# Two edits to a 256-frame hybrid encoder trunk: five weight low parts a layer on GpSimd, and one slice of projections between the sparse branch's output and its split

## The chip, the core and the metric

The kernel runs on one core of one Trainium2 chip. The metric is the device time of one execution in microseconds. The core has five engines with a queue each, served in order: TensorE (PE; PEld is its weight load), VectorE (DVE), ScalarE (ACT), GpSimd (POOL) and SyncE (SP), which issues most DMAs. An instruction waits on semaphores for what it needs; whatever stands behind it in its queue waits too.

## The reference

Two layers over x of 256 x 1024 in float32. A layer normalises x, projects it with one matrix `w_in`, feeds three token mixers (A: gated linear attention, GLA; B: sparse attention over 64 keys chosen by an indexer, DSA; C: differential attention), multiplies each by a SiLU gate, projects each to 1024, merges them by sigmoid gates and adds an output projection to x.

```python
proj = h @ w_in[l]
(gq, gk, gv, ga, gz, bq, bk, bv, iq, ik, iw, bz,
 cq, ck, cv, cz, gate) = jnp.split(proj, SPLIT_AT, axis=-1)
y_a = _gla(...) * jax.nn.silu(gz)
y_b = _dsa(...) * jax.nn.silu(bz)
y_c = _diff(...) * jax.nn.silu(cz)
g = jax.nn.sigmoid(gate.reshape(B, T, N_BRANCH, D_MODEL))
merged = sum(g[:, :, i] * (y @ w_br[l, i]) for i, y in enumerate((y_a, y_b, y_c)))
x = x + merged @ w_out[l]
```

## The kernel before, in words

Every product is made to float32 precision from three matmuls (`mm3`, line 279): each operand is split into a high part that TensorE reads exactly and a low part, the rest; high by high, high by low and low by high are summed in PSUM. A matmul is recorded under lines 124 (products) and 127 (transposes).

Weights come in units of 128 x 1024 (two row blocks of 512 columns). `Stream` (line 184) keeps their order, one list `PLAN` per layer, made from `ORDER` (line 35): bq, cq, ck, gate2, cz, bk, cv, gq, iq, bv, gv, gz, bz, gate0, gate3, gate4, then `br0`, the pair gate5 and gate1 (seven products `q1` to `q7`, by a scheme that saves one of eight), `br1` and the output. Each of the plain projections has four units. `load` (line 199) has SP fetch a unit into one of four `raw` buffers; `split` (line 227) makes the unit's high part `whi` on ScalarE and its low part `wlo` on VectorE, each in one of six buffers. So a raw buffer is loaded again when both parts are made, and a `whi` buffer is written again when TensorE has done the unit six before. Some units of the pair are sums of two, made by DMAs that GpSimd issues (line 211).

`project` (line 344) runs a projection unit by unit: for each half unit it issues the matmuls for both blocks of 128 frames (six, or a slice), and then `flow.pump()` (line 259). `Flow` holds the mixers' work as generators; each `yield n` in one says that its next piece is issued n slices later. So a generator's work is spread between the projections' matmuls. What comes of this is only the order in which the program is written: a scheduler then sets each engine's queue, by that order and by its own estimate of what is ready when.

A projection's accumulators, one for each block of frames, stand in four PSUM buffers called `pj`; what the mixers make in PSUM stands in four others, `at`. The gates' accumulators come free by a tanh on ScalarE (line 1102).

The parts that the argument touches, in the order of a layer's stage from gz to br0:

- `dsa_attend` (line 699): logits `blog`, on VectorE masked by `ns` (line 709) and reduced to the negative row maximum `negm` (711), exponentials `bp` with row sums on ScalarE (678), then a reciprocal `rs` and four scalings on VectorE (717, 720), transposes `pT` on TensorE and their split `bpT` (730, 731).
- `gla_task` (line 875): its output `go` is squared on ScalarE (905), normalised by GpSimd's `v` and `r` (286, 287), scaled by VectorE to `ya` (912), and transposed and split (`yT`, `yTh`, `yTl`).
- `dsa_out` (line 735): two products `av`, each scaled by `bz` to `yb` on VectorE (747) and split to `ybh` (ScalarE) and `ybl` (VectorE).
- `branches` (line 951): `br0` projects the three mixers' outputs in the order A, C, B.

Of the kernel before, what the change touches and what calls it, by code (L numbers as in the profile page):

```python
# [8 lines left out]
F32 = mybir.dt.float32  # L9
F32R = mybir.dt.float32r  # L10
BF16 = mybir.dt.bfloat16
AF = mybir.ActivationFunctionType
# [38 lines left out]
PLAN, USE = [], {}  # L51
# [28 lines left out]
plan()  # L80
NPLAN = len(PLAN)
SUMS_AHEAD = 10


def columns(*widths):
# [21 lines left out]
def trunk(ctx: ExitStack, tc: tile.TileContext, x0, x1, units, wsmall, pack, ptmp, wa2b, out):  # L107
    nc = tc.nc
    V, A, G = nc.vector, nc.scalar, nc.gpsimd
# [32 lines left out]
    def w2(shape, dt=F32, n="w2"):  # L142
        return sp.tile(shape, dt, tag="w2", bufs=BUFS["w2"], name=nm(n))
# [16 lines left out]
    def at(shape, n="at"):  # L160
        return pp.tile(shape, F32, tag="at", bufs=4, name=nm(n))
# [8 lines left out]
    HV = [slice(h * 512, h * 512 + 512) for h in range(2)]  # L170
# [13 lines left out]
    class Stream:  # L184
# [42 lines left out]
        def split(self):  # L227
            j = len(self.made)
            self.begin_sum(j + SUMS_AHEAD)
            raw, (hi, lo) = self.raws[j], self.tiles()  # L230
            self.splits[j] = (A.activation(hi, raw, AF.Copy), V.tensor_sub(lo, raw, hi.bitcast(F32)))  # L231
            what, *arg = PLAN[j % NPLAN]
            if what in ("t1", "t2"):
                self.add(j // NPLAN, "t2" if what == "t1" else "t4", *arg)
            if j in self.after:
                self.hold(j, self.after[j])
# [42 lines left out]
    def mm3(ps, lh, ll, rh, rl, first, last):  # L279
        TE.matmul(ps, lh, rh, start=first, stop=False)  # L280
        TE.matmul(ps, lh, rl, start=False, stop=False)
        TE.matmul(ps, ll, rh, start=False, stop=last)
# [132 lines left out]
    def yT(y):  # L415
        ps = at([P, 4, P], "yT")
        for b in range(4):
            TE.transpose(ps[:, b], y[:, b * P:(b + 1) * P], ident)
        return [[a[:, k] for k in range(4)] for a in split(ps, [P, 4, P], "yT", kp)]
# [117 lines left out]
    for l in range(L):  # L537
# [151 lines left out]
        def transposed_probs(pt, h0, per, t, pT):  # L689

            ps = at([P, per, t + 1, P], "pT")
            for j in range(per):
                for s in range(t + 1):
                    TE.transpose(ps[:, j, s], pt[:, j, s * P:(s + 1) * P], ident)
            hi, lo = split(ps, [P, per, t + 1, P], "pT")
            for j in range(per):
                pT[h0 + j] = [(hi[:, j, s], lo[:, j, s]) for s in range(t + 1)]
# [37 lines left out]
        def dsa_out():  # L735

            his, los = [], []
            for hp in range(2):
                o = at([P, 2, T], "av")
                for j in range(2):  # L740
                    h = 2 * hp + j
                    hs = slice(h * P, h * P + P)
                    v = [(a[:, hs] for a in val["bv"][s]) for s in range(2)]
                    mm3(o[:, j], *v[0], *(a[:, h] for a in bpT[0]), True, False)
                    mm3(o[:, j, P:], *v[1], *(a[:, h] for a in bpT[1]), False, True)
                y = w2([P, CH], F32, "yb")
                V.scalar_tensor_tensor(y, o.rearrange("p j t -> p (j t)"), 0.5, val["bz"][hp], op0=OP.mult, op1=OP.mult)
                hi, lo = split(y, [P, CH], "yb", kp)
                his.append(hi.rearrange("p (j t) -> p j t", j=2))
                los.append(lo.rearrange("p (j t) -> p j t", j=2))  # L750
                yield 1
            for t in range(2):
                yTs[1, t] = [[a[h // 2][:, h % 2, tts[t]] for h in range(4)] for a in (his, los)]
                flow.done.add(f"y1{t}")

        def dsa_task():
            flow.start(dsa_out(), Y["by"], {"bp0", "bp1", "bv", "bz"})
            yield from dsa_index(0)
            flow.start(dsa_attend(0), Y["att0"], {"bq0", "bk0"})
            yield from dsa_index(1)  # L760
            flow.start(dsa_attend(1), Y["att0"], {"bq1", "bk0", "bk1"})
# [355 lines left out]
        for h, n, t in ((0, 0, 0), (0, 0, 1), (0, 1, 0), (0, 1, 1), (1, 0, 0), (1, 1, 0), (1, 0, 1), (1, 1, 1)):  # L1117
# [3 lines left out]
            for ps, c in cols:  # L1121
                for k in range(4):
                    wh, wl = ws.need(use(l, f"out{n}{h}")[k // 2])
                    hi, lo = mT[h, t]
# [90 lines left out]
```

## Time and profile before

| | before |
|---|---|
| median of 3 runs | 601.38 us (601.23 to 602.41) |
| the profiled execution | 602.52 us |
| its span, first to last instruction | 600.8 us |
| mean granted TensorE clock in it | 0.996 |
| TensorE busy with matmuls | 590.5 us (98%) |
| VectorE, ScalarE, GpSimd busy | 476.5, 366.9, 78.6 us |

Times in the rows below are microseconds from the span's start. The busy time of TensorE is a union of intervals that overlap, since a matmul's shown duration (0.39 us for 512 columns) is longer than the distance to the next. So a stop of TensorE is best read from the distance of two starts. A wait is put down to what ended last before it.

### The profile page before, as it was taken

To read this page: it belongs to the slowest core of one execution; us is meant where nothing else is said; L and a number is where in the kernel's file an instruction comes from. 1 tells how busy PE (TensorE), PEld (TensorE's weight loads), DVE (VectorE), ACT (ScalarE), POOL (GpSimd) and SP (SyncE) were. 2 spreads that over 40 slices of the span, in tenths; PEclk is the share of its full clock that TensorE was granted. 3 is DMA by queue.
4 is the path that set the end of the run, shared out by engine and by line. 5 is a ranking of instruction groups with operands and counts; after the bars stand their busy time and mean duration, and the time that the engine had idled before them with its cause. 6 is when DMAs were issued, how large, how long until landed. Compare 5 with 4: busy or idle time off the path is not lost. (4 is left out here: it accounts for less than half of the span.)

```text
span 600.8 us, 8806 instructions
## 1 busy us (share of the span) xinstructions
PE 590.5 (98%) x3142; PEld 500.8 (83%) x3142; DVE 476.5 (79%) x785; ACT 366.9 (61%) x633; POOL 78.6 (13%) x111
## 2 busy tenths in 40 slices
PE   8999999999999998999999999999999999899997
PEld 4888888998899887888878888889888988788886
DVE  6878997766999865899586799676879987679971
ACT  5759875765736555764566788576674545558630
POOL 6034101000011112100010240201000021101000
PEclk9999999999999999999999999999999999999999
DMA  8664566434535997877546455632636198869621
GB/s 343 212 230 141 153 218 190 142 107 173 175 107 195 281 269 161 203 252 239 179 129 208 156 168 166 221 128 90 212 107 207 59 310 303 181 194 238 208 85 71
DMA packets 31148, 111.35 MB, mean 185 GB/s; under 512 B 3456, under 2 KB 3840, under 8 KB 31104
## 3 DMA queue, kind: packets, MB, share of 16 engines
q1 hardware_dynamic: 28800, 102.39, 51.1%
q0 software_dynamic: 2304, 8.39, 8.1%
q8 instruction: 25, 0.41, 0.3%
q14 instruction: 19, 0.16, 0.1%
HBM read 109.72 MB, written 1.05 MB: 184 GB/s over the span
## 5 line engine op out<-in xcount | busy, mean ns | idle before, releaser
L231 ACT ACTIVATE whi<-raw 128x1024 fp32r<-128x1024 f32 x176 | 185.1, 1063 | 110.1 <-issue 25.4
L231 DVE TENSOR_TENSOR wlo<-raw,whi 128x1024 fp32r<-128x1024 f32 x176 | 213.6, 1226 | 41.9 <-ACT whi L231 40.7
L124 PE MATMUL gate<-whi,hTh 128*128 128x512 f32 x128 | 50.7, 396 | 0.7 <-ACT gate L1102 0.7
L124 PE MATMUL gate<-wlo,hTh 128*128 128x512 f32 x128 | 50.7, 396 | 0.0
L124 PE MATMUL gate<-whi,hTl 128*128 128x512 f32 x128 | 49.5, 390 | 0.0
L287 POOL TENSOR_TENSOR r<-v,half 128x4 f32<-128x4 f32 (+1 forms) x24 | 33.7, 1406 | 2.0
L286 POOL TENSOR_SCALAR v<-ss 128x4 f32<-128x4 f32 (+1 forms) x24 | 8.0, 335 | 174.0 <-DVE ss L389 99.5
L211 POOL DMA_DIRECT2D sum<-in_units x16 | 14.2, 888 | 120.7 <-DMA sum<-in_units 55.9
L124 PEld LDWEIGHTS gate<-whi,hTh 128*128 128x128 f32 x128 | 24.1, 188 | 6.2 <-ACT gate L1102 1.6
L124 PE MATMUL br<-whi,yTh 128*128 128x512 f32 x64 | 25.1, 393 | 3.4 <-ACT gate L1102 3.4
L124 PEld LDWEIGHTS gate<-whi,hTl 128*128 128x128 f32 x128 | 24.1, 188 | 4.8
L124 PEld LDWEIGHTS gate<-wlo,hTh 128*128 128x128 f32 x128 | 24.1, 188 | 4.4
L124 PE MATMUL out<-whi,mTh 128*128 128x512 f32 (+1 forms) x72 | 26.7, 371 | 0.0
L124 PE MATMUL out<-wlo,mTh 128*128 128x512 f32 (+1 forms) x72 | 26.3, 366 | 0.0
L124 PE MATMUL out<-whi,mTl 128*128 128x512 f32 (+1 forms) x72 | 26.2, 366 | 0.0
L124 PE MATMUL br<-wlo,yTh 128*128 128x512 f32 x64 | 24.9, 390 | 0.0
L124 PE MATMUL br<-whi,yTl 128*128 128x512 f32 x64 | 24.9, 389 | 0.0
L231 DVE TENSOR_TENSOR wlo<-sum,whi 128x1024 fp32r<-128x1024 f32 x16 | 19.2, 1219 | 5.0 <-ACT whi L231 5.0
L231 ACT ACTIVATE whi<-sum 128x1024 fp32r<-128x1024 f32 x16 | 17.0, 1061 | 9.1 <-PE br L124 5.7
L124 PE MATMUL iq<-hTh,whi 128*128 128x256 f32 x64 | 18.7, 292 | 0.0
L124 PE MATMUL iq<-hTl,whi 128*128 128x256 f32 x64 | 18.4, 288 | 0.0
L124 PE MATMUL bz<-hTh,whi 128*128 128x256 f32 x64 | 18.4, 287 | 0.0
(351 smaller groups left out, 1682.8 us busy)
## 6 DMA issues: line engine op xcount, KB each, us to landing
raw<-in_units SPq DMA_DIRECT2D x180, 512.0 KB, 4.2
sum<-in_units POOLq DMA_DIRECT2D x16, 512.0 KB, 7.2
sum<-in_units SPq DMA_DIRECT2D x8, 512.0 KB, 5.7
wsr<-in_wsmall SPq DMA_DIRECT2D x2, 416.0 KB, 7.7
xe<-in_x SPq DMA_DIRECT2D x1, 584.0 KB, 3.4
x<-in_x SPq DMA_DIRECT2D x1, 512.0 KB, 7.7
out<-xe SPq DMA_DIRECT2D x2, 256.0 KB, 2.2
pt<-in_ptmp SPq DMA_DIRECT2D x1, 384.0 KB, 9.2
```

The lines of the kernel that those rows point to most:

```text
L124: return self.put(nc.tensor.matmul(*a, **k))
L211: G.dma_start(self.sums[l, "t3" if what == "t3" else "t1", pair, i], units[u + i], accum_op=OP.add)
L231: self.splits[j] = (A.activation(hi, raw, AF.Copy), V.tensor_sub(lo, raw, hi.bitcast(F32)))
L286: G.tensor_scalar(v, ss, 1.0 / dim, EPS, op0=OP.mult, op1=OP.add)
L287: G.tensor_tensor(r, v, half[:, :n], op=OP.pow)
```

## The change

There are two edits. In `split`, for five units of each layer (the second of gz, bz, gate0 and gate3, the first of gate4) the low part is made by GpSimd in two halves of 512 columns, instead of by VectorE in one. In `dsa_out` a `yield 1` stands between the scaling `yb` and its split, so that the split is written a slice of projections later. The second edit also puts the whole second product of `dsa_out` a slice later.

```diff
+POOL_LO = [USE[c][i] for c, i in (("gz", 1), ("bz", 1), ("gate0", 1), ("gate3", 1), ("gate4", 0))]
...
-            self.splits[j] = (A.activation(hi, raw, AF.Copy), V.tensor_sub(lo, raw, hi.bitcast(F32)))
             what, *arg = PLAN[j % NPLAN]
+            a = A.activation(hi, raw, AF.Copy)
+            if j % NPLAN in POOL_LO:
+                self.splits[j] = (a,)
+                for h in HV:
+                    G.tensor_sub(lo[:, h], raw[:, h], hi[:, h].bitcast(F32))
+            else:
+                self.splits[j] = (a, V.tensor_sub(lo, raw, hi.bitcast(F32)))
...
                 V.scalar_tensor_tensor(y, o.rearrange("p j t -> p (j t)"), 0.5, val["bz"][hp], op0=OP.mult, op1=OP.mult)
+                yield 1
                 hi, lo = split(y, [P, CH], "yb", kp)
```

The lines behind the edits move down by 5 to 12 in the changed kernel (1102 becomes 1114). The scheduler's order changes in three places of each layer. The number behind a name tells one buffer from the next; it is a few higher in the changed kernel for the same thing.

The first place is ScalarE's queue while TensorE ends gate3. `gate_2425<-gate_546` is the tanh of gate0's first block, `gate_2427` of its second. Before:

```order
L231 ACTIVATE whi_1829<-raw_1827 128x1024
L231 ACTIVATE whi_1853<-raw_1851 128x1024
L730 ACTIVATE bpT_228<-pT_2211 128x4x128
L678 ACTIVATE bp_2354,sums_2325<-blog_2345,negm_2326 128x256 x2
L293 ACTIVATE yTh_2404<-yT_2399 128x512
L1102 ACTIVATE gate_2425<-gate_546_2311 128x512
L231 ACTIVATE whi_1887<-raw_1885 128x1024
L1102 ACTIVATE gate_2427<-gate_547_2312 128x512
L730 ACTIVATE bpT_228<-pT_2442 128x2x128
```

With the change:

```order
L237 ACTIVATE whi_1834<-raw_1832 128x1024
L689 ACTIVATE bp_2359,sums_2330<-blog_2350,negm_2331 128x256 x2
L304 ACTIVATE yTh_2409<-yT_2404 128x512
L237 ACTIVATE whi_1858<-raw_1856 128x1024
L741 ACTIVATE bpT_228<-pT_2216 128x4x128
L1114 ACTIVATE gate_2430<-gate_546_2316 128x512
L1114 ACTIVATE gate_2432<-gate_547_2317 128x512
L237 ACTIVATE whi_1892<-raw_1890 128x1024
L741 ACTIVATE bpT_228<-pT_2447 128x2x128
```

The exponentials and `yTh` moved ahead of one split and of `bpT`, and the second tanh ahead of another. On TensorE, at the same place, the transposes of the probabilities and of `ya` stood twenty matmuls into gate4 (before):

```order
L124 MATMUL gate_597_2567<-whi_1829,hTh 128x512
L124 MATMUL gate_597_2567<-wlo_1830,hTh 128x512
L127 MATMUL pT_2442<-xe,bp_2336 128x128 x4
L127 MATMUL pT_2457<-xe,bp_2354 128x128 x4
L127 MATMUL yT_2510<-xe,ya_2266 128x128 x4
L124 MATMUL gate_598_2568<-whi_1720,hTh 128x512
```

and stand now between gate3 and gate4 (`gate_593` is gate4's first accumulator here):

```order
L129 MATMUL gate_572_2435<-wlo_1707,hTh 128x512
L129 MATMUL gate_572_2435<-whi_1706,hTl 128x512
L132 MATMUL pT_2447<-xe,bp_2341 128x128 x4
L132 MATMUL pT_2462<-xe,bp_2359 128x128 x4
L132 MATMUL yT_2515<-xe,ya_2271 128x128 x4
L129 MATMUL gate_593_2553<-whi_1724,hTh 128x512
```

They moved ahead by twenty matmuls; the number of instructions up to the end of br0 is the same.

The second place is ScalarE's queue at the end of gate4. `gate_571` and `gate_572` are gate3's accumulators, `gate_597` and `gate_598` (now `gate_593` and `gate_594`) gate4's. Before:

```order
L231 ACTIVATE whi_2021<-sum_1678 128x1024
L293 ACTIVATE ybh_2534<-yb_2532 128x512
L293 ACTIVATE ybh_2559<-yb_2557 128x512
L231 ACTIVATE whi_2058<-sum_1699 128x1024
L1102 ACTIVATE gate_2563<-gate_571_2429 128x512
L1102 ACTIVATE gate_2565<-gate_572_2430 128x512
L1102 ACTIVATE gate_2639<-gate_597_2567 128x512
L1102 ACTIVATE gate_2641<-gate_598_2568 128x512
```

With the change:

```order
L304 ACTIVATE ybh_2545<-yb_2537 128x512
L1114 ACTIVATE gate_2549<-gate_571_2434 128x512
L1114 ACTIVATE gate_2551<-gate_572_2435 128x512
L304 ACTIVATE ybh_2588<-yb_2580 128x512
L237 ACTIVATE whi_2026<-sum_1682 128x1024
L1114 ACTIVATE gate_2644<-gate_593_2553 128x512
L237 ACTIVATE whi_2063<-sum_1703 128x1024
L1114 ACTIVATE gate_2646<-gate_594_2554 128x512
```

Gate3's two tanhs moved between the two splits of `yb`, and the splits of the summed units behind them.

The third place is GpSimd's queue during gate0 and gate3. `wlo_1664` and `wlo_1725` are the low parts of gate3's and gate4's unit, `v` and `r` the two GLA normalisers. Before:

```order
L674 MEMSET ns_1897 64x64
L211 DMA sum_1678<-in_units 128x1024
L211 DMA sum_1699<-in_units 128x1024
L286 TENSOR_SCALAR v_2200<-ss_2194 128x4
L287 TENSOR_TENSOR r_2201<-v_2200,half 128x4
L674 MEMSET ns_2235 64x64
L286 TENSOR_SCALAR v_2260<-ss_2254 128x4
L287 TENSOR_TENSOR r_2261<-v_2260,half 128x4
```

With the change:

```order
L685 MEMSET ns_1902 64x64
L241 TENSOR_TENSOR wlo_1664<-raw_1661,whi_1663 128x512 x2
L216 DMA sum_1682<-in_units 128x1024
L216 DMA sum_1703<-in_units 128x1024
L297 TENSOR_SCALAR v_2205<-ss_2199 128x4
L298 TENSOR_TENSOR r_2206<-v_2205,half 128x4
L685 MEMSET ns_2240 64x64
L241 TENSOR_TENSOR wlo_1725<-raw_1722,whi_1724 128x512 x2
L297 TENSOR_SCALAR v_2265<-ss_2259 128x4
L298 TENSOR_TENSOR r_2266<-v_2265,half 128x4
```

Two pairs of halves were put in, one ahead of the DMAs of the sums, one ahead of the second normaliser. SP's order is the same in both kernels.

## Rows read from the trace of the kernel before

**Rows 1.** The page, busy time by engine, share of the span, count of instructions.

```profile
PE 590.5 (98%) x3142; PEld 500.8 (83%) x3142; DVE 476.5 (79%) x785; ACT 366.9 (61%) x633; POOL 78.6 (13%) x111
```

**Rows 2.** Waits of TensorE: total us, times, longest us.

```profile
PE br L124 <- ACT gate L1102: 3.4, 2, 1.7
PE gate L124 <- ACT gate L1102: 0.7, 2, 0.4
```

**Rows 3.** Timeline, TensorE, layer 0: start, duration, instruction [idle before, releaser].

```profile
210.81 0.39 PE L124 MATMUL gate<-whi,hTl 128*128 128x512 f32 x1
211.56 0.50 PE L124 MATMUL gate<-whi,hTh 128*128 128x512 f32 x1 [0.36 <-ACT gate L1102]
211.90 0.40 PE L124 MATMUL gate<-wlo,hTh 128*128 128x512 f32 x1
...
226.53 0.39 PE L124 MATMUL gate<-whi,hTl 128*128 128x512 f32 x1
228.60 0.50 PE L124 MATMUL br<-whi,yTh 128*128 128x512 f32 x1 [1.68 <-ACT gate L1102]
```

**Rows 4.** Timeline, ScalarE, ahead of the first stop.

```profile
208.08 1.06 ACT L231 ACTIVATE whi<-raw 128x1024 fp32r<-128x1024 f32 x1 [1.67 <-PE gate L124]
209.04 0.58 ACT L730 ACTIVATE bpT<-pT 128x512 fp32r<-128x512 f32 x1
209.52 0.47 ACT L678 ACTIVATE bp<-blog,negm 128x256 f32<-128x256 f32 x1
...
210.42 0.60 ACT L293 ACTIVATE yTh<-yT 128x512 fp32r<-128x512 f32 x1
210.90 0.61 ACT L1102 ACTIVATE gate<-gate 128x512 f32<-128x512 f32 x1
```

**Rows 5.** Timeline, ScalarE, ahead of the second stop.

```profile
225.02 0.63 ACT L293 ACTIVATE ybh<-yb 128x512 fp32r<-128x512 f32 x1 [1.89 <-DVE yb L747]
...
227.97 2.04 ACT L1102 ACTIVATE gate<-gate 128x512 f32<-128x512 f32 x4
```

**Rows 6.** Groups by shape: count, busy us, mean ns of one, idle before.

```profile
L231 DVE TENSOR_TENSOR wlo<-raw,whi 128x1024 fp32r<-128x1024 f32 x176 | 213.6, 1226 | 41.9 <-ACT whi L231 40.7
...
L483 POOL TENSOR_TENSOR wlo<-raw,whi 128x512 fp32r<-128x512 f32 x2 | 2.8, 1420 | 1.7 <-ACT whi L479 1.7
...
L287 POOL TENSOR_TENSOR r<-v,half 128x4 f32<-128x4 f32 x16 | 18.2, 1135 | 1.3
```

**Rows 7.** Timeline, SP's load behind gate4's low part; ScalarE's split after it.

```profile
198.75 0.33 SPq L206 DMA_DIRECT2D raw<-in_units  x1
...
199.85 1.06 ACT L231 ACTIVATE whi<-raw 128x1024 fp32r<-128x1024 f32 x1 [2.38 <-DMA raw<-in_units]
```

**Rows 8.** Timeline, TensorE's transposes in gate3 and gate4.

```profile
208.06 0.60 PE L127 MATMUL yT<-xe,ya 128*128 128x128 f32 x4
...
216.27 1.03 PE L127 MATMUL pT<-xe,bp 128*128 128x128 f32 x8
...
217.50 0.48 PE L124 MATMUL gate<-whi,hTh 128*128 128x512 f32 x1
```

**Rows 9.** Timeline, VectorE from a low part to the scaled probabilities.

```profile
204.81 1.22 DVE L231 TENSOR_TENSOR wlo<-raw,whi 128x1024 fp32r<-128x1024 f32 x1
...
208.31 0.69 DVE L711 TENSOR_REDUCE negm<-blog 128x2 f32<-128x512 f32 x1
...
211.66 1.13 DVE L720 TENSOR_SCALAR bp<-bp,rs 128x256 f32<-128x256 f32 x4
```

**Rows 10.** Timeline, GpSimd and VectorE side by side.

```profile
170.88 1.09 POOL L1111 TENSOR_TENSOR gz<-gz,pk 128x512 f32<-128x512 f32 x1 [3.21 <-DVE gz L412]
...
171.31 1.74 DVE L231 TENSOR_TENSOR wlo<-raw,whi 128x1024 fp32r<-128x1024 f32 x1
```

**Rows 11.** Timeline, VectorE and TensorE: a later unit, made and first used.

```profile
249.96 1.22 DVE L231 TENSOR_TENSOR wlo<-sum,whi 128x1024 fp32r<-128x1024 f32 x1
...
255.25 0.39 PE L124 MATMUL q<-wlo,sh 128*128 128x512 f32 x1
```

## The prediction

> **What bounds the kernel now.** I read the page first: TensorE is busy 590.5 of 600.8 us, VectorE 79%, GpSimd 13% [rows 1]. A change that only relieves VectorE can give nothing here unless VectorE's lateness reaches TensorE, so the second view is what TensorE itself waited for. Past the start-up, in the first 20 us of the span, it has two kinds of wait, each twice, once per layer: a `br` matmul for the tanh of line 1102 (3.4 us in two times) and a `gate` matmul for the same line (0.7 us in two) [rows 2]. The timeline gives their size and place in layer 0. Matmuls of 512 columns start 0.23 us apart. Between 210.81 and 211.56 the distance is 0.75, so 0.52 is lost; between 226.53 and 228.60 it is 2.07, so 1.84 is lost [rows 3]. (The wait column is smaller because a matmul's shown duration overlaps the next.) The matmul behind the first stop follows at 211.90 - 211.56 = 0.34 instead of 0.23, another 0.1, and I take the same for the second stop. That is 2.57 us a layer, 5.1 in all, and nearly all that this stage can give.
>
> Both are waits for a PSUM buffer: an accumulator of `pj` comes free when ScalarE has done the tanh on it. In neither case was the tanh short of data. It stood late in ScalarE's queue. At the first stop ScalarE did a split that waited for TensorE, the copy `bpT`, the softmax exponentials `bp` and `yTh`, and only then gate0's tanh, 210.90 to 211.51 [rows 4]. At the second it waited for VectorE's `yb`, made both `ybh`, one more split, and then four tanhs in a row from 227.97; TensorE went on at 228.60, when the first was done [rows 3, 5].
>
> **The change part by part.** *The low parts.* Five of 96 low parts a layer leave VectorE: 5 x 1.226 = 6.1 us less there. GpSimd makes each in two halves of 1.42, 2.84 a unit, 14.2 a layer [rows 6], on an engine that is 87% idle. TensorE does not need them soon. The gate4 unit's low part ended on VectorE just before 198.75, when SP sent the next load into its raw buffer [rows 7]; 1.226 earlier, at 197.5, its high part was there. Its first use is the matmul at 211.90 [rows 3]. GpSimd's will be ready at 197.5 + 2.84 = 200.3: 11.6 us are left. The other four stand in the same ring of six, about as far ahead. What is queued behind: that load of SP's now goes at 200.3, 1.6 us later. Its user is the split that started at 208.08 because TensorE released its buffer then, not because the load landed [rows 4]; in the new order that split stands behind `yTh`, at 209.1. The load took at most 208.08 - 198.75 = 9.3 us, so it lands by 209.6 at the latest, and 0.5 us at worst reaches the tanh. SP's own order is unchanged. I cost the loads at nothing; the cover is the 1.1 us of the next paragraph.
>
> *The order at the first stop.* With VectorE's work shorter, the scheduler puts the second half of the exponentials and `yTh` ahead of the split, gate0's two tanhs together behind `bpT`, and moves eight transposes `pT` and four `yT` from the middle of gate4 to its front. TensorE reaches that point at 210.81 + 0.23 = 211.04, and twelve transposes take 217.50 - 216.27 = 1.23 [rows 8], so gate4's first matmul is due at 212.27. ScalarE: `yTh` follows the transposes `yT`, ending near 208.7 [rows 8]; then steps as in [rows 4], 0.48 for `yTh`, 0.96 for the split, 0.48 for `bpT`, 0.61 for the tanh: 211.2. That is 1.1 us before it is wanted, so the 0.52 goes.
>
> The transposes brought forward need the scaled probabilities at 211.04. VectorE's low part of 204.81 stays where it was, since it waits for its load, and ends at 206.03; the row maximum takes 0.69 (206.7), the four exponentials' pair 210.42 - 209.52 = 0.90 on ScalarE (207.6), beside them one low part of 1.23 (207.95), a small reciprocal (0.2 allowed), four scalings 1.13: 209.3 [rows 4, 6, 9]. Spare: 1.8 us. This is what is late next if VectorE or GpSimd is slower than I think.
>
> *The slice between.* In `dsa_out` the first `ybh` is now followed by gate3's tanhs, and the second split comes after them. Even with the first `ybh` where it was, 225.02, a tanh 0.5 later ends near 226.1, before TensorE's 226.76. With the transposes 5.2 us earlier, `av` and `yb` come some 4 us earlier too, so the margin is above 3 us. The 1.84 goes, and would with either half of the change. Nothing is queued behind the moved split that TensorE wants: `yb` is used last of the three branches.
>
> *Two read ports.* At 171.31 a low part on VectorE took 1.74 instead of 1.226 while GpSimd worked from 170.88 to 171.97: 0.51 lost in 0.66 of overlap, about 0.8 us per us [rows 6, 10]. If both gate3's and gate4's GpSimd work (2 x 2.84) lay wholly beside such VectorE work, VectorE would lose 4.5, less the 2.5 it no longer does: 2.1 late, 0.3 past the spare, 0.6 us in two layers. Bounds for this term: 0 and 0.6 us; I take 0, because at 197.5 to 200.3 VectorE mostly waits for a split that starts at 199.85 [rows 7]. The Trainium skill (GPSIMD Engine Reference, Specifications) says that GpSimd's SBUF interfaces are "Shared with VectorE (contention with DVE instructions in a 2-port perf mode or with two SBUF inputs)", which speaks against moving a two-input subtract there. The row at 171.31 agrees with it; by the rule at full strength the sum would be 4.3 instead of 4.9.
>
> **Sum.** Gains 2 x (0.52 + 1.84) = 4.7, up to 5.1 with the slow second matmuls; one such follows the transposes anyway, so 4.9. The profiled execution took 602.52 (span 600.8); by it the new one is 597.6. It lies 1.1 above the median of the three runs, 601.38, so against the median: 596.5.
>
> **Rivals.**
> 1. *Supply.* TensorE comes 2.5 us sooner to `br0`, and loads cannot. For it: it is the stage with the most transfers. Against: the unit with the least spare that I found later has its low part done at 251.18 and used at 255.25, 4.1 us [rows 11], more than 2.5. If half were given back: 599.0.
> 2. *The change doesn't do what it says at `br0`:* `yb` comes so late that gate3's tanh, now behind the first `ybh`, still ends after TensorE's 226. For it: `ybh` did wait for `yb` [rows 5]. Against: the margin above. Only 2 x 0.6 is won: 600.1.
> 3. *GpSimd's queue takes the place (slower).* The second GLA normaliser `v`, `r` now stands behind gate4's low part on GpSimd; VectorE waits in order for `r`, and behind it are the mask, the maximum and the scalings that `pT` needs. With 2.84 for the pair, `r` (1.135) [rows 6] ends near 201.7, before the split of 199.85 and its low part let VectorE go on anyway (202.1); 0.4 + 1.8 us are spare. From a pair of 5.0 us on TensorE waits, and from 7.6 on all 2.57 are lost. At 10 us it is 2.4 slower a layer: 606.2. Against: both pieces of GpSimd's subtract in the trace average 1.42.
> 4. *Nothing moves:* the order on the engines already contradicts it; 601.4.
>
> **Numbers.** Forecast 0.76, rival 1 0.09, rival 2 0.06, rival 3 0.06, rival 4 0.03. A measurement here tells about 0.2%, 1.2 us, which is also the spread of the three runs. The range runs from 595.7 (5.1 won, and the lowest run is 0.15 under the median) to 599.4, rival 1 included and rivals 2 to 4 (0.15) left out. Faster 0.90 (forecast, rival 1, most of rival 2), same 0.05, slower 0.05.
>
> **What would show it.** Right: TensorE's waits lose both lines 1102 (now 1114); the distances before gate4 and before `br0` fall to 0.23 after a transpose or matmul; ScalarE's first gate tanh ends by 211.3, gate3's by about 223; GpSimd gains 20 halves near 1.4 us, about 28 us busy; VectorE's busy time falls by about 12. Wrong: a wait of TensorE for `bp` at 211 (rival 3 or the ports), GpSimd halves of 2.5 us and more, or a stop before `br0` that stays.

## The result and the profile after

| | before | after |
|---|---|---|
| median | 601.33 us (601.23 to 602.41, 4 runs) | 596.16 us (595.94 to 596.52, 4 runs) |
| the profiled execution, its span | 602.52, 600.8 us | 595.94, 594.2 us |
| mean granted TensorE clock in it | 0.996 | 1.000 |

The ratio is 0.9911, with a 95% interval of 0.9893 to 0.9928: 5.2 us faster, where 4.9 was forecast. The page of after, busy time by engine:

```profile
PE 587.7 (99%) x3142; PEld 499.8 (84%) x3142; DVE 471.1 (79%) x775; ACT 367.0 (62%) x633; POOL 108.2 (18%) x131
```

Against [rows 1], GpSimd has 29.6 us more and VectorE only 5.4 us less, though ten low parts of 1.226 us left it. What TensorE waited for in after:

```profile
PE bq L129 <- DVE wlo L494: 1.3, 2, 0.7
...
```

Both lines of [rows 2] are gone (the tanh would now be L1114). Three other kinds of wait are left: 1.2 us before the first matmul, 0.6 and 0.2 later; the largest lie in the first 20 us. The timeline of TensorE in after, at the places of [rows 3]; the start-up was 1.3 us shorter, so times here are about 1.3 us ahead of those of before:

```profile
209.53 0.39 PE L129 MATMUL gate<-whi,hTl 128*128 128x512 f32 x1
209.75 1.03 PE L132 MATMUL pT<-xe,bp 128*128 128x128 f32 x8
210.63 0.60 PE L132 MATMUL yT<-xe,ya 128*128 128x128 f32 x4
210.98 0.48 PE L129 MATMUL gate<-whi,hTh 128*128 128x512 f32 x1
211.30 0.39 PE L129 MATMUL gate<-wlo,hTh 128*128 128x512 f32 x1
...
224.60 0.39 PE L129 MATMUL gate<-whi,hTl 128*128 128x512 f32 x1
224.82 0.39 PE L129 MATMUL br<-whi,yTh 128*128 128x512 f32 x1
```

The transposes follow the last gate3 matmul at 0.22 us, gate4's first matmul follows them, and `br0` follows gate4 at 0.22. The slow second matmul after the transposes (0.32) is there as forecast. ScalarE in after, to compare with [rows 4, 5]:

```profile
208.39 0.59 ACT L741 ACTIVATE bpT<-pT 128x512 fp32r<-128x512 f32 x1
208.87 1.08 ACT L1114 ACTIVATE gate<-gate 128x512 f32<-128x512 f32 x2
...
219.87 0.63 ACT L304 ACTIVATE ybh<-yb 128x512 fp32r<-128x512 f32 x1 [1.89 <-DVE yb L758]
220.41 1.07 ACT L1114 ACTIVATE gate<-gate 128x512 f32<-128x512 f32 x2
221.36 0.63 ACT L304 ACTIVATE ybh<-yb 128x512 fp32r<-128x512 f32 x1
```

gate0's tanhs begin 2.1 us before gate4's first matmul at 210.98, gate3's 4.4 us before `br0`. What GpSimd did with the low parts, one of VectorE's instructions beside them, and `f`, which waits for `r`:

```profile
155.78 3.10 POOL L241 TENSOR_TENSOR wlo<-raw,whi 128x512 fp32r<-128x512 f32 x2 [9.55 <-ACT whi L237]
...
196.26 2.54 POOL L241 TENSOR_TENSOR wlo<-raw,whi 128x512 fp32r<-128x512 f32 x2 [0.93 <-ACT whi L237]
199.16 1.87 POOL L298 TENSOR_TENSOR r<-v,half 128x4 f32<-128x4 f32 x1
...
156.34 1.38 DVE L668 SCALAR_TENSOR_TENSOR acc<-relu,iws,acc 128x128 f32<-128x128 f32 x1
...
201.07 0.17 DVE L920 TENSOR_SCALAR f<-r 128x4 f32<-128x4 f32 x1 [0.91 <-POOL r L298]
```

A pair took 2.54 us where VectorE was idle for most of the time, and 3.10 beside a busy one. An `acc` of VectorE's took 1.38 us and the two `ns` of 128 columns 1.20 each, where in before they average 0.34 and 0.23.

### The profile page after: what moved, and what is told of

It is laid out like the page before. It is cut to its first block, busy times and chain, and to the rows that moved or that the text cites. A ratio compares the mean times of both kernels' runs of the same rounds, so it can differ in the third digit from the quotient of the medians.

```text
span 594.2 us, 8820 instructions
## 1 busy us (share of the span) xinstructions
PE 587.7 (99%) x3142; PEld 499.8 (84%) x3142; DVE 471.1 (79%) x775; ACT 367.0 (62%) x633; POOL 108.2 (18%) x131
## 4 chain that ended last, share of the span: by engine, by line
PE 97%; DVE 1%; DMA 1%; ACT 0%; issue 0%; POOL 0%; DVEq 0%; POOLq 0%
PE gate L129 15%; PE br L129 11%; PE out L129 7%; PE q L129 6%; PE bz L129 4%; PE iq L129 4%; PE gz L129 4%; PE gv L129 4%; PE cz L129 4%; PE ck L129 4%; PE gq L129 4%; PE cv L129 4%; PE bv L129 4%; PE bk L129 4%; PE bq L129 3%; PE cq L129 3%
## 5 line engine op out<-in xcount | busy, mean ns | idle before, releaser
L243 DVE TENSOR_TENSOR wlo<-raw,whi 128x1024 fp32r<-128x1024 f32 x166 | 201.3, 1226 | 48.5 <-ACT whi L237 47.7
L241 POOL TENSOR_TENSOR wlo<-raw,whi 128x512 fp32r<-128x512 f32 x20 | 28.4, 1439 | 43.5 <-ACT whi L237 43.2
L298 POOL TENSOR_TENSOR r<-v,half 128x4 f32<-128x4 f32 (+1 forms) x24 | 35.5, 1477 | 2.0
```

The lines of the kernel that those rows point to most:

```text
L241: G.tensor_sub(lo[:, h], raw[:, h], hi[:, h].bitcast(F32))
L243: self.splits[j] = (a, V.tensor_sub(lo, raw, hi.bitcast(F32)))
L298: G.tensor_tensor(r, v, half[:, :n], op=OP.pow)
```

## Experiments

Three theories stood against each other. **A**: the place of the gate tanhs in ScalarE's queue made both stops, and a lighter VectorE earns nothing by itself. **B**: the gain is the work that left VectorE. **C**: each edit removes one stop. The kernel before ran beside each group of runs, with medians from 601.37 to 601.54 us.

**The slice alone.** The kernel before with the one line of `dsa_out`.

```diff
                 V.scalar_tensor_tensor(y, o.rearrange("p j t -> p (j t)"), 0.5, val["bz"][hp], op0=OP.mult, op1=OP.mult)
+                yield 1
                 hi, lo = split(y, [P, CH], "yb", kp)
```

> Theory A (the place of the gate tanhs in ScalarE's queue made both stops; lighter VectorE earns nothing by itself): with the slice alone gate3's tanhs stand between the two ybh, so the stop of 1.84 us before br0 goes, with its slow second matmul 1.94 a layer, 3.9 in all; the stop of 0.52 before gate4 stays, since ScalarE's order there is that of before. 601.3 - 3.9 = 597.4 us. Theory B (the gain comes from the 12 us of VectorE work that moved to GpSimd): no low part moves here, so at most the small slip of the split is felt: 600.5 to 601.5 us, and both stops are seen.

Measured: 597.70 us, ratio 0.9934 (0.9922 to 0.9947). Timeline of TensorE at both places:

```profile
210.15 0.39 PE L124 MATMUL gate<-whi,hTl 128*128 128x512 f32 x1
210.90 0.50 PE L124 MATMUL gate<-whi,hTh 128*128 128x512 f32 x1 [0.36 <-ACT gate L1103]
...
225.86 0.39 PE L124 MATMUL gate<-whi,hTl 128*128 128x512 f32 x1
226.09 0.39 PE L124 MATMUL br<-whi,yTh 128*128 128x512 f32 x1
```

The first stop is there (0.75 instead of 0.23), the second gone, as theory A has it. B falls, since no low part moved and 3.8 us were won.

**The low parts alone.** The change without the `yield 1`.

> The five low parts on GpSimd without the slice. Theory A: ScalarE's queue has the order of the changed kernel at the first stop, and at the second both ybh stand ahead of gate3's tanhs, but yb comes some 4 us earlier than before, so both stops go: 596.2 us, the same as the whole change within 0.5. Theory B: nearly all of the gain too, 596 to 597 us. A theory C, that each edit removes one stop (the slice the one before br0, the low parts the one before gate4): 601.3 - 2 x 0.62 = 600.1 us.

Measured: 596.17 us, 0.9909 (0.9896 to 0.9923), the whole gain. No wait of TensorE for a gate tanh is left. C falls: the low parts remove both stops, and beside them the slice is worth nothing that can be measured. ScalarE ahead of `br0`:

```profile
220.47 0.63 ACT L304 ACTIVATE ybh<-yb 128x512 fp32r<-128x512 f32 x1 [1.89 <-DVE yb L758]
221.26 0.64 ACT L304 ACTIVATE ybh<-yb 128x512 fp32r<-128x512 f32 x1 [0.16 <-DVE yb L758]
221.81 1.06 ACT L1113 ACTIVATE gate<-gate 128x512 f32<-128x512 f32 x2
```

Gate3's tanhs still stand behind both `ybh` here, though no longer behind the split of a summed unit, 0.97 us that could not have made up for 1.84. They are in time because the first `ybh` runs at 220.47 instead of 225.02 [rows 5] (some 3.9 us earlier, the shorter start-up taken off): `br0` begins at 225.42, 3.1 us after the first tanh. So theory A as worded is too narrow for the second stop: it goes if the tanh is put ahead of the second `ybh`, or if `yb`, which both `ybh` wait for, is made earlier.

**Order by an edge, no low part moved.** The slice alone, and an edge that puts the second pair of exponentials behind gate0's first tanh on ScalarE.

```diff
-                    softmax_rows(ps, j, S, prob[h0][:, j], negm, sums, h0 + j)
+                    last["bp"] = softmax_rows(ps, j, S, prob[h0][:, j], negm, sums, h0 + j)
+                    if (t, h0 + j) == (1, per):
+                        last["bp2"] = last["bp"]
...
-                    A.activation(th[int(c[4]), t], ps_[t], AF.Tanh, scale=0.5)
+                    a = A.activation(th[int(c[4]), t], ps_[t], AF.Tanh, scale=0.5)
+                    if c == "gate0" and t == 0:
+                        order(last["bp2"], a)
```

> All low parts stay on VectorE; the slice stays, and one ordering edge puts the second pair of exponentials bp behind gate0's first tanh on ScalarE. That tanh then follows yTh and would run at about 210.0 to 210.6 instead of 210.90 to 211.51, before TensorE's 211.04. Theory A: both stops go with no relief of VectorE at all: 596.3 us, as the whole change. Theory B: VectorE is as loaded as before, 600 us or more.

Measured: 597.85 us, 0.9934 (0.9920 to 0.9947): neither theory's number. ScalarE and TensorE ahead of `br0`:

```profile
224.68 0.63 ACT L293 ACTIVATE ybh<-yb 128x512 fp32r<-128x512 f32 x1 [2.10 <-DVE yb L749]
225.22 0.58 ACT L1105 ACTIVATE gate<-gate 128x512 f32<-128x512 f32 x1
...
225.01 0.44 PE L124 MATMUL gate<-whi,hTl 128*128 128x512 f32 x1
225.85 0.50 PE L124 MATMUL br<-whi,yTh 128*128 128x512 f32 x1 [0.39 <-ACT gate L1105]
```

The first stop went, with VectorE as loaded as before: around 211 TensorE's matmuls start 0.23 us apart. But the second pair of exponentials ran 0.87 us later than with the slice alone, and the scheduler put `pT` 25 matmuls into gate4 instead of 20. By the traces' own times `pT` came 0.35 us and the first `ybh` 0.32 us later, while TensorE was ahead by the stop that it had saved. So the tanh behind the first `ybh` ended at 225.80 where TensorE was due at 225.24: 0.61 us lost at the second place. What was won at one place was given back at the other. That both stops can go without moving a low part is therefore not shown.

**Two units, three units.** The change with the low parts of gate3 and gate4 alone on GpSimd, and with those of gz, bz and gate0 alone.

```diff
-POOL_LO = [USE[c][i] for c, i in (("gz", 1), ("bz", 1), ("gate0", 1), ("gate3", 1), ("gate4", 0))]
+POOL_LO = [USE[c][i] for c, i in (("gate3", 1), ("gate4", 0))]
```

> The change with two low parts a layer on GpSimd instead of five (the second of gate3, the first of gate4). ScalarE's queue has both gate0 tanhs together behind bpT, as with five. Theory A: the same time as the whole change, 596.2 us within 0.5. Theory B: two fifths of the relief and so about two fifths of the gain, 599.3 us. VectorE's busy time would be about 4.9 us less than before less what it waits for GpSimd.

> The change with three low parts a layer on GpSimd (the second of gz, bz and gate0) and none of gate3 or gate4; the slice stays. ScalarE's queue has the order of before at the first stop and gate3's tanhs between the two ybh at the second. Theory A (place in ScalarE's queue): as the slice alone, 597.7 us within 0.4, with the stop of 0.52 us before gate4 still there, although VectorE is relieved of more than in the run with two units, which took 596.5. Theory B (relief of VectorE counts): less than 596.5 us.

Measured: with two 596.50 us, 0.9921 (0.9908 to 0.9933); with three 597.40, 0.9931 (0.9916 to 0.9946), and TensorE still stops before gate4:

```profile
209.63 0.39 PE L129 MATMUL gate<-whi,hTl 128*128 128x512 f32 x1
210.37 0.50 PE L129 MATMUL gate<-whi,hTh 128*128 128x512 f32 x1 [0.36 <-ACT gate L1114]
```

By the medians, more low parts moved won less, and the three are worth little beside the slice alone (597.70). The two intervals overlap; the stop in the trace is the firmer sign. With these two the scheduler puts gate0's tanhs together behind `bpT`, with the three others it leaves them where they stood. The medians differ by 0.9 us, close to two stops of 0.52. Why these two turn the schedule was not tried further.

**How the two engines hold each other up.** Each low part as one GpSimd instruction, and as four.

```diff
-                for h in HV:
-                    G.tensor_sub(lo[:, h], raw[:, h], hi[:, h].bitcast(F32))
+                G.tensor_sub(lo, raw, hi.bitcast(F32))
```

> The change with each of the five low parts as one GpSimd instruction of 1024 columns instead of two of 512. Theory L (a VectorE instruction with its inputs in SBUF waits until GpSimd's running instruction ends): VectorE's longest acc, 1.38 us in the changed kernel against 0.34 alone, may grow up to about 0.34 + 2.5 = 2.9 us, and the sum of VectorE's busy time grows. Theory S (the two share a rate): an acc or ns takes at most about twice its time alone, 0.7 and 0.5 us, whatever the piece. For the time both stops stay away, since ScalarE's queue again has both gate0 tanhs behind bpT: 596.2 us, up to 597 if VectorE's waits of 2.5 us reach pT.

> The change with each of the five low parts as four GpSimd instructions of 256 columns. Theory L: VectorE waits for at most one quarter, about 0.65 to 0.7 us, so its longest acc falls to about 1.0 us. Theory S: as with halves, 1.4 us. ScalarE's queue has both gate0 tanhs even ahead of bpT, so both stops stay away: 596.2 us within 0.5.

Measured: 596.51 us, 0.9919 (0.9904 to 0.9933), and 596.45, 0.9914 (0.9900 to 0.9929): no difference in time. The longest `acc` of VectorE's, with one piece, and then with four:

```profile
156.31 2.91 POOL L240 TENSOR_TENSOR wlo<-raw,whi 128x1024 fp32r<-128x1024 f32 x1 [9.70 <-ACT whi L237]
...
156.87 2.50 DVE L667 SCALAR_TENSOR_TENSOR acc<-relu,iws,acc 128x128 f32<-128x128 f32 x1
```

```profile
156.20 3.43 POOL L241 TENSOR_TENSOR wlo<-raw,whi 128x256 fp32r<-128x256 f32 x4 [9.28 <-ACT whi L237]
...
158.11 0.92 DVE L668 SCALAR_TENSOR_TENSOR acc<-relu,iws,acc 128x128 f32<-128x128 f32 x1
```

2.50, 1.38 and 0.92 us for pieces of 1024, 512 and 256 columns: the instruction waits for the piece that is running and then takes its 0.34. Theory L holds and S falls. In the first fence GpSimd ends at 159.22 and VectorE at 159.37, so VectorE's own 0.34 began about 0.2 before GpSimd's shown end. The Trainium skill (SBUF — State Buffer, SBUF: two separate sides) says it so: the one that starts first has the shared pair of ports for the whole instruction and the other "fully blocks". These rows agree; the last section has a GpSimd instruction for which the rows do not.

**A late normaliser.** The changed kernel with `r` of the second GLA block made slow, as rival 3 supposes.

```diff
+    def rstd_slow(ss, times):
+        G.tensor_scalar(v16.rearrange("p (a b) -> p a b", a=4), ss.unsqueeze(1).to_broadcast([P, 4, 4]), 1.0 / 128, EPS,
+                        op0=OP.mult, op1=OP.add)
+        for _ in range(times):
+            G.tensor_tensor(r16, v16, half, op=OP.pow)
+        return r16[:, :4]
...
-                r = rstd(ss, 4, 128)
+                r = rstd_slow(ss, 3) if t else rstd(ss, 4, 128)
```

> The changed kernel with the second GLA normaliser made slow: v and r of 16 columns instead of 4 and the power for r made three times over, so that r ends some 6.6 us later (three times about 2.86 us, by r's 1.03 for 4 and 1.64 for 8 columns, instead of 1.87). Rival 3 of the prediction (VectorE waits in order for r, and what pT needs stands behind it; 2 us to spare, then one for one): 4.5 us lost a layer, 605 us. Against it: the schedule is made anew, and it now puts one or two splits and r's users later and the first tanhs behind the exponentials; then only the exponentials (about 209 to 211) hold the tanh up, a stop of about 1 us a layer before gate4: 598 us.

Measured: 606.58 us (605.83 to 609.19), ratio 1.0098 (1.0073 to 1.0124): slower than before. TensorE waits twice for the tanh, 3.0 us each time. The timeline from `r` to the stop:

```profile
199.40 10.10 POOL L307 TENSOR_TENSOR r<-v,half 128x16 f32<-128x16 f32 x3
...
208.04 1.23 DVE L245 TENSOR_TENSOR wlo<-raw,whi 128x1024 fp32r<-128x1024 f32 x1 [1.36 <-ACT whi L239]
209.18 0.68 DVE L751 TENSOR_TENSOR bpT<-pT,bpT 128x512 fp32r<-128x512 f32 x1
209.78 0.16 DVE L929 TENSOR_SCALAR f<-r 128x4 f32<-128x4 f32 x1
209.85 1.28 DVE L731 TENSOR_REDUCE negm<-blog 128x2 f32<-128x512 f32 x2
...
212.46 0.49 ACT L698 ACTIVATE bp<-blog,negm 128x256 f32<-128x256 f32 x1
212.90 1.11 ACT L1123 ACTIVATE gate<-gate 128x512 f32<-128x512 f32 x2
...
209.92 0.66 PE L132 MATMUL yT<-xe,ya 128*128 128x128 f32 x4 [0.29 <-DVE bpT L751]
213.57 0.50 PE L129 MATMUL gate<-whi,hTh 128*128 128x512 f32 x1 [2.99 <-ACT gate L1123]
```

The three powers of 16 columns took 2.90 to 3.75 us, where 2.86 was the estimate, so `r` ended 8.5 us late (209.50 against 201.03). TensorE lost 3.24 us at the tanh and 0.45 ahead of it, 3.7 a layer, and some 1.7 more in layer 0 at a lower clock (last section).

Not `pT` but the tanh was late, behind four exponentials that waited for VectorE's `negm`. `negm` stands in VectorE's queue behind `f`, which needs `r`. But `f` did not wait for `r`: it followed `bpT` at once, 0.28 us after `r` had ended. What the late `r` changed is the order that the scheduler made: `f` and the first `negm`, at 201.07 and 201.15 in the changed kernel, now stand behind three low parts and `bpT`. So the run shows what that order costs. It does not show rival 3's step, VectorE standing still for `r` until `pT` is late. By rival 3's count (2.2 us to spare, then one for one) 8.5 us would cost 6.3 a layer, not 3.7; that the total comes near the 605 us of the expectation is luck, since `r` was 1.9 us later than meant and the clock added its part.

**The start of the program.** TensorE's two stops for `bq` in the first 20 us are waits for low parts that VectorE makes beside GpSimd's. Two kernels make the first four units anew; in the second GpSimd takes no part in them. The changed kernel ran beside them.

```diff
-    lo(0, 1, "G")
+    lo(0, 1, "V")
...
-    hi(1, 0, "G")
-    hi(1, 1, "G")
+    hi(1, 0, "A")
+    hi(1, 1, "A")
...
-    lo(2, 1, "G")
+    lo(2, 1, "V")
...
-    hi(3, 0, "G")
-    hi(3, 1, "G")
+    hi(3, 0, "A")
+    hi(3, 1, "A")
```

(The last four lines are in the second kernel alone. In both, the eight low parts, the `hTl` and the high parts are issued in the order in which TensorE takes them.)

> The changed kernel once more, as the mark for the next two runs on the same chip: 596.2 us.

> The changed kernel with its first four weight units split anew: all eight low parts of 512 columns on VectorE (two were GpSimd's) in the order in which TensorE takes them, the first three units' high parts on ScalarE, the fourth's still a cast on GpSimd. In the changed kernel VectorE's first low part took 1.77 us instead of 0.68 and its third and fourth 2.38 instead of 1.28, beside low parts of GpSimd's; TensorE stopped 0.84 and 0.90 us for them. Theory L (VectorE waits for GpSimd's running instruction): the first stop of 0.84 goes, the second too where no cast falls before a low part; VectorE then has 8 x (0.6 + 0.3) us of work before the next frame block, so about 0.8 us is won of the 1.7: 595.4 us. Against it: GpSimd's two low parts were a real help and VectorE becomes the bound: 596.2 us or more.

> As the last, with the fourth unit's high parts on ScalarE too, so that GpSimd reads nothing while VectorE makes the first eight low parts. Theory L: each of these takes 0.68 us and both stops of TensorE go; ScalarE is then the fullest (eight high parts, eight hTh and the squares, about 7.3 us from 7.1), so 0.8 us won again, 595.4 us, 595.0 to 596.0. Against it: 596.2 us or more.

Measured: the changed kernel 596.27 us, 0.9912 (0.9895 to 0.9928); the first 596.02, 0.9913 (0.9898 to 0.9927); the second 595.17 (595.03 to 596.15), 0.9898 (0.9883 to 0.9913). In the second every one of the eight low parts takes 0.68 or 0.69 us, and TensorE's waits for low parts are gone. It is the fastest kernel here, 1.1 us ahead of the changed one by the medians; the intervals overlap, so the size is less sure than the mechanism. In the first, TensorE waited 0.8 us for one of the casts left on GpSimd, which gave most of it back (its profiled execution is the longest of its four, 597.26 us, with a granted clock of 0.91 in the first 20 us). Both kernels also change the order of these instructions, which was not tried by itself.

## Why the prediction was right

*The two stops.* Right in place, cause and size: 2 x (0.52 + 1.84 + 0.1) = 4.9, measured 5.2, and 5.1 in the repeat. The profiled execution fell by 6.6, more than the runs: its own 1.1 us above the median lay in the start, where TensorE's granted clock was 0.91 over the first 20 us in before and 1.00 in after. Taking the profiled execution's excess off the sum was right.

*The first stop's margin.* Forecast: the first tanh done at 211.2, 1.1 us before its buffer is wanted, and the scaled `bp` 1.8 us before `pT`. Measured: the first tanh done near 209.5, 1.5 us before 210.98; the scalings done at 207.74, 2.0 before `pT`. Of the 1.5, 1.23 are the transposes that now stand ahead of gate4; even without them the tanh would have been done some 0.3 us before TensorE came, and the third run shows that the stop goes with the tanh moved and the transposes left in gate4.

*The second stop.* Forecast: it goes with either half, with over 3 us to spare. Both halves alone removed it. With the whole change the first `ybh` ran 3.9 us earlier, the start-up taken off, where some 4 were forecast for `yb`. The first tanh then had 3.9 us to spare (it ended near 220.95); with the slice alone 0.6, which the edge of the third run then used up.

*The low parts on GpSimd.* 2.84 us a unit was forecast, 2 x 1.439 measured; alone a half takes 1.27. The row from which 1.42 was read had VectorE beside it too.

*Two read ports: the term that failed.* The time's term, 0, was right, but the step behind it, "about 0.8 us per us", was the wrong law, and "VectorE's busy time falls by about 12" came out wrong. The row at 171.31 [rows 10] fits the other law as well: that low part ended at 173.05, so its own 1.226 began at 171.82, 0.15 before GpSimd's shown end, as in the fence above. One row could not tell the two laws apart; three lengths of the piece could. The groups of VectorE in after:

```profile
L243 DVE TENSOR_TENSOR wlo<-raw,whi 128x1024 fp32r<-128x1024 f32 x166 | 201.3, 1226 | 48.5 <-ACT whi L237 47.7
...
L668 DVE SCALAR_TENSOR_TENSOR acc<-relu,iws,acc 128x128 f32<-128x128 f32 x14 | 7.7, 553 | 0.0
...
L684 DVE TENSOR_TENSOR ns<-ns,nf 128x128 bf16<-128x128 bf16 x2 | 2.4, 1195 | 0.1
...
L683 DVE TENSOR_SCALAR nf<-acc 128x256 bf16<-128x256 f32 x2 | 2.3, 1168 | 0.1
```

and the same three small ones in before:

```profile
L657 DVE SCALAR_TENSOR_TENSOR acc<-relu,iws,acc 128x128 f32<-128x128 f32 x14 | 4.8, 344 | 0.0
L672 DVE TENSOR_SCALAR nf<-acc 128x256 bf16<-128x256 f32 x2 | 0.6, 319 | 0.1
...
L673 DVE TENSOR_TENSOR ns<-ns,nf 128x128 bf16<-128x128 bf16 x2 | 0.5, 226 | 0.1
```

The low parts fell by 12.3 us (213.6 to 201.3), as forecast; these three groups rose by 6.5. A wait for GpSimd is shown as busy time, and falls on whatever small instruction comes next: an `ns` took five times its 0.23. (The `nf` stood beside GpSimd's multiplication of `gz`, which in before had held up the low part at 171.31.) TensorE waited for none of them, so it cost nothing that can be seen. It works the other way too: `r`, begun beside a low part that ran from 198.93 to 200.16, took 1.87 us instead of the 1.03 of the first normaliser's, and VectorE waited 0.91 for it, where rival 3's working had left 0.4 spare; the spare ahead of `pT` covered that.

*Rivals 1 and 3.* Of rival 1 nothing was seen: TensorE has no wait for a load or a low part behind the start. Of rival 3 the first half was seen, VectorE's wait of 0.91 us for `r`, within the spare. Whether a longer one would reach `pT` at rival 3's price is open, since the run with the late normaliser got another order.

*The range.* Its lower end does not follow from what is said of it: 601.38 - 5.1 - 0.15 is 596.1, not 595.7, and its upper end lies 0.4 above rival 1's 599.0 without a reason. The measured 596.16 lies inside either way.

*Which edit did it.* The prediction gave the first stop to the low parts and the second to either. Shown by the runs of one edit each. It treated the five low parts as one relief. Beside the slice two suffice, and three others do not.

## What to carry to other kernels

A stop for a buffer is cured at the instruction that frees it: look at what stands ahead of that one in its engine's queue, and at what those instructions wait for. Judge an edit by what it does there, not by how much work it moves (two low parts removed a stop that three others left). Where a schedule is made anew after each edit, read the margin at the next stop as well, since what is late there gives the gain back. In these rows VectorE and a two-input subtract of GpSimd's take turns by whole instructions. Shorter pieces made the longest wait shorter (2.50, 1.38, 0.92 us); in that place it changed no time. At the start, where TensorE does wait for VectorE's low parts, taking GpSimd away from beside them won 1.1 us by the medians.

## What was not expected

*Who starts first decides.* In two executions of the changed kernel the order at the start differs: in the first GpSimd's low part began 0.05 us ahead of VectorE's, in the second 0.05 behind.

```profile
6.69 1.27 POOL L494 TENSOR_TENSOR wlo<-raw,whi 128x512 fp32r<-128x512 f32 x1 [0.79 <-ACT whi L490]
...
6.74 1.77 DVE L494 TENSOR_TENSOR wlo<-raw,whi 128x512 fp32r<-128x512 f32 x1
```

```profile
7.01 1.78 POOL L494 TENSOR_TENSOR wlo<-raw,whi 128x512 fp32r<-128x512 f32 x1 [0.89 <-ACT whi L490]
...
6.96 0.69 DVE L494 TENSOR_TENSOR wlo<-raw,whi 128x512 fp32r<-128x512 f32 x1
```

The loser took 1.77 or 1.78 us, and either could be it.

*A power does not hold VectorE up.* In the run with the late normaliser GpSimd made powers from 199.40 to 209.50. Three low parts of VectorE's began in that time, the last at 208.04 (shown there), and took 1.22 or 1.23 us, as alone. The other way round the wait is there: the two powers that began 0.97 and 0.54 us before a running low part ended took 3.75 and 3.30 us, the third, 0.09 before, 2.90. So the turns by whole instructions are shown here for GpSimd's subtracts and multiplication, and not for a power once it runs; the sentence of the Trainium skill cited above makes no such difference.

*The clock after a stop.* In the run with the late normaliser TensorE stood for 3.24 us in each layer. Windows of 4.5 us after each stop (the columns are the busy time of the five engines, then granted clock, DMA share and GB/s):

```profile
213.50:218.00 4.50, 4.43 (x12) 3.53 (x13) 1.63 (x6) 0.51 (x2) 0.91 (x1) 0.62 0.94 210
509.50:514.00 4.50, 4.46 (x19) 3.68 (x20) 1.59 (x6) 0.47 (x1) 0.91 (x1) 1.00 1.00 220
```

In layer 0 the clock was granted at its lower level, 1.2 of 2.4 GHz, for most of the window (0.62 on average, matmuls 0.43 us apart instead of 0.23); in layer 1, after the same stop, at the upper one throughout. What tells the two apart is left open.
